# A hybrid attention and recurrence layer on one core: row spreads through DRAM in place of a matmul, and the first gate maps loaded at a written place

## The chip, the cores and the metric

The kernel runs on one NeuronCore of a Trainium2 chip. Its time is device time in microseconds (us) for one execution. The median of three runs before the change is 661.3 us (661.18 to 662.85). The core has five engines with queues of their own: TensorE (in the profile PE, its weight loads PEld), VectorE (DVE), ScalarE (ACT), GpSimd (POOL) and SyncE (SP, which here only issues transfers). Transfers are issued by SP, ACT or POOL and carried out by 16 DMA engines. An engine works its queue in order, and an instruction that waits holds up what is queued behind it on that engine.

## The reference, cut to what matters

One layer of an encoder over 512 tokens of width 2048, in float32. Three places of it need one factor per token, an inverse root of a mean square:

```python
def rms_norm(x, w):
    xf = x.astype(jnp.float32)
    y = xf * lax.rsqrt(jnp.mean(xf * xf, axis=-1, keepdims=True) + EPS)
    return (y * w.astype(jnp.float32)).astype(x.dtype)
...
    h = rms_norm(x, norm_w)
    proj = jnp.einsum('bsd,de->bse', h, w_in)
    q, k, v, g_attn, xr, g_lru = jnp.split(proj, SPLITS, axis=-1)
    attn_out = attention_group(q, k, v, q_norm_w, k_norm_w)
    lru_out = lru_group(xr, conv_w, conv_b, lru_wa, lru_ba, lru_wx, lru_bx, lru_lambda)
    mixed = jnp.concatenate([rms_norm(attn_out, attn_norm_w) * jax.nn.silu(g_attn),
                             rms_norm(lru_out, lru_norm_w) * jax.nn.silu(g_lru)], axis=-1)
    return x + jnp.einsum('bse,ed->bsd', mixed, w_out)
```

`lru_group` is a short convolution along the tokens, then two linear recurrences (forward and backward) whose gates come from block-diagonal 128x128 maps `lru_wa` and `lru_wx`, eight blocks in each direction. `attention_group` is attention of 8 query heads and 2 key heads of 128 with norms and a rotation.

## The kernel before, in words

Products are made from float32 values split in a high and a low part, three matmuls for each product (`mm3`, L144 to L147). A weight block of 256 rows by 512 columns (512 KB) is loaded into one of three raw buffers (`wraw`, L187, transfer at L193) and split by ScalarE (high part, L204) and VectorE (low part, L205); a raw buffer comes free when its split is done. A projection whose output features lie on the partitions (`proj_feat`, L278) holds four accumulators `pj` of 128x512 and runs over eight chunks c of 256 input rows; a step (c, e) is one chunk into accumulator e, six matmuls. A second projection of the kind takes the same four accumulator banks over, so its first matmul on bank e waits until the first one's bank e has been read.

The input is used without its own norm factor. x is loaded in chunks (L223), turned by TensorE (L230), scaled by the gain and split (L232, L233), and its squares are summed per token on VectorE (`xsquare`, L239). The factor `rstd` per token goes on later, when accumulators are emptied: `evac_bc` (L360 to L368) multiplies bank e, which has features on the partitions and tokens along the row, by `rbc`, a 128x512 tile that has the 512 factors on every partition.

Three times a column form of factors, [128, 4] with token 128 t + p at (p, t), has to become such a tile. That is `rows` (L262): VectorE makes four products of the identity with a column (L265), which gives a 128x512 tile with the factors on diagonals, TensorE multiplies a matrix of ones with it in float32 (L267), and VectorE copies the accumulator out (L268). The three calls:

- `xstats` (L270 to L274): VectorE adds up the sums (L272), GpSimd forms the root with two operations (`rsqrt_mean`, L256 and L257), and `rows` fills `rbc`. It is called in the main loop over the first projection's steps behind step (7, 0) (L969 to L971).
- in `kv` (L546 to L548): the squares of the recurrence output are summed over the features by `group_rstd` (L639 to L651), matmuls of 128x128 with one column of ones (L644), for two halves of `hsum`; VectorE copies the four columns out (L649), GpSimd forms the root `r_l`, four steps later `rows` fills `gbc`. `normed` (L655, L656) multiplies the recurrence outputs `hs` by it.
- at L1042, behind the attention: the same for the attention's one sum (`asum`) and root `r_a`, into the same `gbc`; L656 multiplies the attention outputs `av` by it.

The recurrence comes in two halves of four blocks (`lru_half`, L370). It first loads its four pairs of gate maps (L376 and L377, 128 KB each) into buffers of tag `k2`, then empties the accumulators with `evac_bc` (L366), and for each pair of blocks runs the split of the maps (L391, L392), the convolution (L396, L401), the gate matmuls, and the scans. `weave` mixes the next projection's steps into this chain.

What sets the order: TensorE's order is as written for the whole kernel. SP's is as written up to the end of the first projection (`s1`, closed at L973) and in the last stage, ScalarE's and VectorE's as written until step (1, 2) (`s2`, L964) and in the last stage, GpSimd's as written during the attention. Everywhere else a planner puts the instructions of an engine in order at build time, by a priority (`high_priority`) and modelled times. The gate maps of the first half are issued by `lru_half` behind L973, with a high priority, so the planner places them on SP's queue.

Of the kernel before, what the change touches and what calls it, by code (L numbers as in the profile page):

```python
# [1 line left out]

# [8 lines left out]
F32 = mybir.dt.float32  # L11
F32R = mybir.dt.float32r
AF = mybir.ActivationFunctionType
ALU = mybir.AluOpType
AX = mybir.AxisListType

P = 128
SEQ = 512
DM = 2048
KT = DM // P  # L20
NT = SEQ // P
# [34 lines left out]
def hybrid_kernel(  # L56
# [20 lines left out]
    nc = tc.nc  # L77
# [4 lines left out]
    pools, order = {}, {"left": [], "right": []}  # L82

    def opened(name, side):
        pools[name] = tc.alloc_tile_pool(name=name, bufs=1, side=side, reuse_waits="tile")
        order[side].append(name)
        return pools[name]
# [16 lines left out]
    dp = ctx.enter_context(tc.tile_pool(name="dp", bufs=1, space=bass.MemoryType.DRAM))  # L104
# [3 lines left out]
    def nm(s):  # L108
        cnt[0] += 1
        return f"{s}_{cnt[0]}"  # L110
# [4 lines left out]
    def work():  # L115
        return ("lru", LRU_K2, LRU_B4) if "lru" in pools else ("att", ATT_K2, ATT_B4)

    def k2(dt=F32, shape=(P, SEQ)):
        pool, n, _ = work()
        return pools[pool].tile(list(shape), dt, tag="k2", bufs=n, name=nm("k2"))  # L120
# [14 lines left out]
    def mm():  # L135
        return ps.tile([P, SEQ], F32, tag="mm", name=nm("mm"))

    def const(shape, name, dt=F32):
        return cp.tile(list(shape), dt, tag=name, name=name)

    def f(ap):
        return ap.bitcast(F32)
# [7 lines left out]
    ident = const([P, P], "ident")  # L150
    make_identity(nc, ident)
    ones = const([P, P], "ones")
# [64 lines left out]
    def xload(c, nk=1):  # L217

        xc = b4(shape=(P, NT, 2 * P))
        for k in range(nk):  # L220
            ks = slice(k * 2 * P // nk, (k + 1) * 2 * P // nk)
            cs = slice(c * 2 * P + ks.start, c * 2 * P + ks.stop)
            nc.sync.dma_start(xc[:, :, ks], xf[:, cs].rearrange("(t p) d -> p t d", p=P))  # L223
            yield xc

    def xturn(xc, kk):
        pt = mm()
        for t in range(NT):
            ks = slice(kk % 2 * P, (kk % 2 + 1) * P)
            nc.tensor.transpose(pt[:, t * P : (t + 1) * P], xc[:, t, ks], ident)  # L230
        xh[kk], xl[kk] = x2(), x2()
        nc.scalar.activation(xh[kk], pt, AF.Identity, scale=nw[:, kk : kk + 1])  # L232
        nc.vector.scalar_tensor_tensor(  # L233
            xl[kk], pt, nw[:, kk : kk + 1], f(xh[kk]), op0=ALU.mult, op1=ALU.subtract
        )

    def xsquare(xc, c):
        for t in range(NT):
            nc.vector.scalar_tensor_tensor(  # L239
                xc[:, t, :], xc[:, t, :], 1.0, xc[:, t, :], op0=ALU.mult, op1=ALU.mult,  # L240
                accum_out=ssq[:, t, c : c + 1],
            )

    def xchunk(c):
        with tc.high_priority(AHEAD):
            (xc,) = xload(c)
        yield
        with tc.high_priority(AHEAD):
            for k in range(2):
                xturn(xc, 2 * c + k)  # L250
        xsquare(xc, c)
        yield

    def rsqrt_mean(dst, src, n, width):

        nc.gpsimd.tensor_scalar(dst, src, 1.0 / n, EPS, op0=ALU.mult, op1=ALU.add)  # L256
        nc.gpsimd.tensor_tensor(dst, dst, nhalf[:, :width], op=ALU.pow)  # L257

    rstd = const([P, NT], "rstd")
    rbc = const([P, SEQ], "rbc")  # L260

    def rows(dst, col, dg):  # L262

        for t in range(NT):
            nc.vector.tensor_scalar(dg[:, t, :], ident, col[:, t : t + 1], None, op0=ALU.mult)  # L265
        pb = mm()
        nc.tensor.matmul(pb, ones, dg.rearrange("p t q -> p (t q)"), start=True, stop=True)  # L267
        nc.vector.tensor_copy(dst, pb)  # L268

    def xstats():  # L270
        s = const([P, NT], "xsum")
        nc.vector.reduce_sum(s, ssq, axis=AX.X)  # L272
        rsqrt_mean(rstd, s, DM, NT)
        rows(rbc, rstd, k2(shape=(P, NT, P)))  # L274

# [80 lines left out]
    sums = {}  # L358

    def evac_bc(acc):  # L360

        res = []
        with tc.high_priority():
            for a in acc:
                e = ev()
                nc.vector.tensor_mul(e, a, rbc)  # L366
                res.append(e)
        return res  # L368

    def lru_half(half, acc):  # L370

        grs = []
        for n in range(4 * half, 4 * half + 4):
            gr = k2(shape=(P, 4, P))
            with tc.high_priority(AHEAD):
                nc.sync.dma_start(gr[:, 0:2, :], lru_wa[:, n].rearrange("d c e -> c d e"))  # L376
                nc.sync.dma_start(gr[:, 2:4, :], lru_wx[:, n].rearrange("d c e -> c d e"))  # L377
            grs.append(gr)
        xrs = evac_bc(acc)
        for b in range(0, 4, 2):  # L380
            bs = slice(b, b + 2)
            steps = ((6, 4, 8, 4), (10, 5, 8, 5))[half][bs]
            yield from lru_pair(4 * half + b, xrs[bs], grs[bs], steps, 99 if half and b else 0)
# [68 lines left out]
    def lru_squares():  # L452

        hsum = pools["rot"].tile([P, 2, SEQ], F32, tag="hsum", name="hsum")
        nc.scalar.activation(hsum, hp[0], AF.Square)
        for pair in hp[1:]:
            yield 2
            sq = pools["rot"].tile([P, 2, SEQ], F32, tag="hsq", bufs=1, name=nm("hsq"))
            nc.scalar.activation(sq, pair, AF.Square)
            nc.vector.tensor_add(hsum, hsum, sq)  # L460
        sums["l"] = [hsum[:, k, :] for k in range(2)]


    def rope_consts():
# [54 lines left out]
    def turn(rot, h):  # L519

        pt = mm()
        for t in range(NT):
            nc.tensor.transpose(pt[:, t * P : (t + 1) * P], rot[t][:, h, :], ident)  # L523
        return pt

    def split_ps(pt, hi, lo):
        nc.scalar.copy(hi, pt)
        nc.vector.tensor_sub(lo, pt, f(hi))

    def kv(es):  # L530
        rot = norm_rope(es, NKV, rk)
        yield 20
        opened("wx", "right")
        for t in range(NT):
            vv = es[t][:, NKV * HD :]
            vt = pools["qkv"].tile([P, 2, NKV * HD], F32R, tag="v", bufs=NT, name=nm("v"))
            vh[t], vl[t] = vt[:, 0, :], vt[:, 1, :]
            nc.scalar.copy(vh[t], vv)
            nc.vector.tensor_sub(vl[t], vv, f(vh[t]))
        yield from lru_squares()  # L540
        for h in range(NKV):
            yield (16, 4)[h]
            kt = pools["qkv"].tile([P, 2, SEQ], F32R, tag="kt", bufs=NKV, name=nm("kt"))
            kth[h], ktl[h] = kt[:, 0, :], kt[:, 1, :]
            split_ps(turn(rot, h), kth[h], ktl[h])
        r = group_rstd(sums["l"], "r_l", NB * P)  # L546
        yield 4
        rows(gbc, r, pools["rope"].tile([P, NT, P], F32, tag="kv", bufs=NT, name=nm("kv")))  # L548

    def turned(rot, h):  # L550

# [84 lines left out]
    def fin_s(shape=(P, SEQ)):  # L636
        return pools["fin"].tile(list(shape), F32, tag="s", bufs=2, name=nm("s"))
# [15 lines left out]
    gbc = const([P, SEQ], "gbc")  # L653
# [268 lines left out]
    def busy(n):  # L922
        for _ in range(n):
            nc.tensor.matmul(warm[:, : 2 * P], wv[:, :P], wv, start=True, stop=True)
# [10 lines left out]
    with tc.high_priority():  # L935
# [8 lines left out]
        xturn(xc, 0)  # L944
        busy(WARM2)
    chunks = [xchunk(c) for c in range(1, KT // 2)]
    loads, turns = iter(chunks), iter(chunks)
    for step in proj_feat(C_XR, a1, first, given):
        if step is None:
            with tc.high_priority():  # L950
                first.append(wsplit(raw, 1))
                xturn(xc, 1)
            xsquare(xc, 0)
            next(next(loads), None)
            given[1] = wload(w_in, 2 * P, C_XR)
            continue
        c, e = step
        if (e == 0 or e == 2) and c:
            next(next(loads, iter(())), None)
        if (e, c) == (2, 0) or (e == 1 and c) or (e, c) in ((3, 1), (3, 2)):  # L960
            next(next(turns, iter(())), None)
        if (c, e) == (1, 2):
            given[2] = wload(w_in, 4 * P, C_XR)
            s2.close()  # L964
        if (c, e) == (2, 3):
            vec_load()
        if (c, e) == (5, 3):
            columns(vec, vec_st)
        if (c, e) == (KT // 2 - 1, 0):  # L969
            with tc.high_priority():  # L970
                xstats()  # L971

    s1.close()  # L973
    lru_consts()
# [28 lines left out]

    fill = both()
    weave(fill, kv(kvs))
    drain(fill)

# [29 lines left out]
    r = group_rstd([sums["a"]], "r_a", NH * HD)  # L1037
    closed("att", "qkv")
    opened("fin", "right")
    for _ in range(3):  # L1040
        next(fill)
    rows(gbc, r, fin_s((P, NT, P)))  # L1042


    def build(i, pair, where):
# [22 lines left out]
    acc = []  # L1068
# [74 lines left out]
```

## Time and profile before

| | |
|---|---|
| runs before | 661.18, 661.3, 662.85 us; median 661.3 |
| profiled execution | 660.07 us, of which 658.3 us are its span, first to last instruction |
| mean granted TensorE clock | 0.998 of full speed |
| matmuls L145 to L147 and L891, the weight products | 376 of each of the three kinds at some 0.39 us recorded in the projections with features on the partitions, 192 of each in the others, 672 in the output |
| GpSimd | 14% busy, 121 instructions |
| transfers | 96.17 MB, mean 146 GB/s |

How the lines of a profile are read: a group line names the source line, the engine, the operation, `out<-in` tiles, the shape and type, the count, then busy time and mean duration in ns. A timeline line has the start in us from the span's start, the duration in us, the engine, the line and the operation; in brackets stands how long the engine had been idle and what ended that. "Lq" engines such as SPq are the issuing queues. A line in the list of waits names who waited for whom, then us in total, the number of times and the longest. For transfers the line gives the count, KB each, and the median us from issue to landing. Matmuls are pipelined, so that a recorded matmul of 0.39 us overlaps the next one, which starts 0.23 us after it.

### The profile page before, as it was taken

What the parts mean: (1) busy time and instruction counts of PE and PEld (TensorE: products, weight loads), DVE (VectorE), ACT (ScalarE), POOL (GpSimd) and SP (SyncE); (2) the same over time, 40 slices, a digit from 0 to 9 for tenths busy, and PEclk for the clock granted to TensorE, in tenths of its full rate; (3) what the DMA queues carried; (4) which work ended last, traced back from release to release, by engine and by line L of the source; (5) the groups of instructions that cost most, each with busy time, mean ns of one, the idle gap of its engine ahead of it and who ended that gap; (6) DMA issues with size and microseconds to landing.
All of it is one profiled execution on the core that took longest, in us unless ns stands there. A gap on an engine that the chain in (4) does not pass through costs nothing.

```text
span 658.3 us, 8625 instructions
## 1 busy us (share of the span) xinstructions
PE 651.0 (99%) x2971; PEld 534.1 (81%) x2971; DVE 488.2 (74%) x843; ACT 345.6 (53%) x639; POOL 92.1 (14%) x121
## 2 busy tenths in 40 slices
PE   8999999999999999999999999999999999999997
PEld 6888888888888888888888888888888888888875
DVE  5879688977687952855955568439958998698994
ACT  3533898489856515453744446435444564334441
POOL 0000000000022301233443335410000000000000
PEclk9999999999999999999999999999999999999999
DMA  8843252322334321346875768663355766585322
GB/s 291 288 131 93 65 167 65 97 64 67 93 121 135 92 69 32 102 143 154 179 186 138 192 141 199 158 140 95 96 177 199 259 210 237 189 293 181 132 77 96
DMA packets 52731, 96.17 MB, mean 146 GB/s; under 512 B 4184, under 2 KB 14544, under 8 KB 52560
## 3 DMA queue, kind: packets, MB, share of 16 engines
q1 hardware_dynamic: 45648, 75.17, 36.1%
q0 software_dynamic: 6720, 19.93, 13.1%
q10 hardware_dynamic: 320, 0.53, 0.3%
q8 instruction: 23, 0.38, 0.2%
q14 instruction: 20, 0.16, 0.1%
HBM read 91.42 MB, written 20.97 MB: 171 GB/s over the span
## 4 chain that ended last, share of the span: by engine, by line
PE 96%; DVE 1%; DMA 1%; issue 1%; ACT 0%; ACTq 0%; DVEq 0%
PE pj L145 20%; PE pj L147 20%; PE pj L146 20%; PE mm L891 12%; PE pj L891 9%; PE mm L145 3%; PE mm L147 3%; PE mm L146 3%; PE mm L575 2%; PE mm L230 1%; PE pj L287 1%; PE mm L523 1%; DMA nw_st<-in_norm_w_dram 1%; DVE ol L706 0%; DMA rw<-in_w_out_dram 0%
## 5 line engine op out<-in xcount | busy, mean ns | idle before, releaser
L145 PE MATMUL pj<-x,wh 128*128 128x512 f32 x376 | 151.2, 402 | 0.0
L147 PE MATMUL pj<-x,wl 128*128 128x512 f32 x376 | 146.9, 391 | 0.0
L146 PE MATMUL pj<-x,wh 128*128 128x512 f32 x376 | 146.6, 390 | 0.0
L204 ACT CAST wh<-wr 128x512 fp32r<-128x512 f32 x144 | 86.5, 617 | 77.1 <-PE pj L147 28.8
L205 DVE TENSOR_TENSOR wl<-wr,wh 128x512 fp32r<-128x512 f32 x144 | 98.0, 701 | 30.3 <-ACT wh L204 30.3
L147 PEld LDWEIGHTS pj<-x,wl 128*128 128x128 f32 x376 | 70.6, 188 | 15.3
L146 PEld LDWEIGHTS pj<-x,wh 128*128 128x128 f32 x376 | 70.8, 188 | 13.9 <-issue 0.5
L145 PEld LDWEIGHTS pj<-x,wh 128*128 128x128 f32 x376 | 70.7, 188 | 13.8 <-issue 0.5
L145 PE MATMUL pj<-wh,x 128*128 128x512 f32 x192 | 75.6, 394 | 0.0
L147 PE MATMUL pj<-wh,x 128*128 128x512 f32 x192 | 75.2, 392 | 0.0
L146 PE MATMUL pj<-wl,x 128*128 128x512 f32 x192 | 75.1, 391 | 0.0
L705 ACT CAST oh<-rw 128x512 fp32r<-128x512 f32 x94 | 54.8, 618 | 31.6 <-PE mm L891 16.5
L706 DVE TENSOR_TENSOR ol<-rw,oh 128x512 fp32r<-128x512 f32 x94 | 60.5, 685 | 9.7 <-ACT oh L705 8.8
L891 PE MATMUL mm<-ol,mh 128*128 128x512 f32 x128 | 50.3, 393 | 0.5 <-DVE ol L706 0.5
L891 PE MATMUL mm<-oh,mh 128*128 128x512 f32 x128 | 50.2, 392 | 0.0
L891 PE MATMUL mm<-oh,ml 128*128 128x512 f32 x128 | 50.2, 392 | 0.0
L577 ACT CAST pt<-mm 128x512 fp32r<-128x512 f32 x32 | 18.8, 586 | 53.1 <-PE mm L575 53.1
L145 PEld LDWEIGHTS pj<-wh,x 128*128 128x128 f32 x192 | 36.1, 188 | 8.1 <-issue 0.2
L146 PEld LDWEIGHTS pj<-wl,x 128*128 128x128 f32 x192 | 36.1, 188 | 8.0 <-issue 0.2
L147 PEld LDWEIGHTS pj<-wh,x 128*128 128x128 f32 x192 | 36.0, 188 | 7.9
L563 DVE TENSOR_REDUCE mx<-mm 128x1 f32<-128x512 f32 x32 | 22.1, 689 | 24.5 <-PE mm L147 24.0
L891 PE MATMUL pj<-ol,mh 128*128 128x512 f32 x96 | 37.9, 394 | 0.0
(207 smaller groups left out, 1112.0 us busy)
## 6 DMA issues: line engine op xcount, KB each, us to landing
wr<-in_w_in_dram SPq DMA_DIRECT2D x71, 512.0 KB, 3.7
rw<-in_w_out_dram SPq DMA_DIRECT2D x63, 256.0 KB, 3.7
ts<-in_w_out_dram POOLq DMA_DIRECT2D x24, 512.0 KB, 6.7
rw<-ts SPq DMA_DIRECT2D x31, 256.0 KB, 4.6
ts<-ts POOLq DMA_DIRECT2D x8, 512.0 KB, 5.3
xt<-in_x_dram SPq DMA_DIRECT2D x8, 512.0 KB, 8.7
b<-in_x_dram SPq DMA_DIRECT2D x7, 512.0 KB, 7.6
out_dram<-xt POOLq DMA_DIRECT2D x12, 256.0 KB, 3.0
```

What stands on the lines that cost most here:

```text
L145: nc.tensor.matmul(acc, lh, rh, start=start, stop=False)
L146: nc.tensor.matmul(acc, lh, rl, start=False, stop=False)
L147: nc.tensor.matmul(acc, ll, rh, start=False, stop=stop)
L204: nc.scalar.copy(hi, raw[:, k, :])
L205: nc.vector.tensor_sub(lo, raw[:, k, :], f(hi))
L230: nc.tensor.transpose(pt[:, t * P : (t + 1) * P], xc[:, t, ks], ident)
L563: nc.vector.tensor_reduce(mx, sc, axis=AX.X, op=ALU.max, negate=True)
L575: nc.tensor.transpose(pt[:, s * P : (s + 1) * P], p[:, s * P : (s + 1) * P], ident)
L577: nc.scalar.copy(pth[:, :, tt], p3)
L705: nc.scalar.copy(hi, src)
L706: nc.vector.tensor_sub(lo, src, f(hi))
L891: nc.tensor.matmul(bank[name, s], lh[:, a, ts_], rh, start=i == 0 and j == 0, stop=i == 7 and j == 2,)
```

## The change

`rows` loses the diagonal products, the matmul of ones and the 128x512 copy. In their place TensorE turns the [128, 4] column form to [4, 128] with one transpose, VectorE copies that into a small tile `line_sb`, GpSimd stores it to DRAM as one line of 512 values, and a second GpSimd transfer reads that line into all 128 partitions of the target. `xstats` becomes a generator in two parts: the sum and the root are written behind step (6, 0), and `rows` behind (6, 1), where the old call stood behind (7, 0). The loads of the first half's gate maps become a generator too, of which two maps are taken behind (6, 0) and two behind (6, 1), that is in the stretch in which SP's order is as written; the second half's are loaded where they were. In `lru_squares` VectorE adds the two halves of `hsum` into one, so that `group_rstd` has one part to sum over instead of two.

```diff
--- before.py
+++ after.py
@@ -1,3 +1,4 @@
+import itertools
 from contextlib import ExitStack
 
 import numpy as np
@@ -259,19 +260,23 @@
     rstd = const([P, NT], "rstd")
     rbc = const([P, SEQ], "rbc")
 
-    def rows(dst, col, dg):
-
-        for t in range(NT):
-            nc.vector.tensor_scalar(dg[:, t, :], ident, col[:, t : t + 1], None, op0=ALU.mult)
-        pb = mm()
-        nc.tensor.matmul(pb, ones, dg.rearrange("p t q -> p (t q)"), start=True, stop=True)
-        nc.vector.tensor_copy(dst, pb)
+    line_sb = const([NT, P], "line_sb")
+
+    def rows(dst, col):
+
+        pt = mm()
+        nc.tensor.transpose(pt[:NT, :P], col, ident)
+        nc.vector.tensor_copy(line_sb, pt[:NT, :P])
+        line = dp.tile([1, SEQ], F32, tag=nm("line"), bufs=1, name=nm("line"))
+        nc.gpsimd.dma_start(line.rearrange("o (t p) -> (o t) p", p=P), line_sb)
+        nc.gpsimd.dma_start(dst, line.broadcast_to([P, SEQ]))
 
     def xstats():
         s = const([P, NT], "xsum")
         nc.vector.reduce_sum(s, ssq, axis=AX.X)
         rsqrt_mean(rstd, s, DM, NT)
-        rows(rbc, rstd, k2(shape=(P, NT, P)))
+        yield
+        rows(rbc, rstd)
 
 
 
@@ -367,15 +372,20 @@
                 res.append(e)
         return res
 
-    def lru_half(half, acc):
-
-        grs = []
+    gate_maps = {}
+
+    def gate_loads(half):
+
         for n in range(4 * half, 4 * half + 4):
             gr = k2(shape=(P, 4, P))
             with tc.high_priority(AHEAD):
                 nc.sync.dma_start(gr[:, 0:2, :], lru_wa[:, n].rearrange("d c e -> c d e"))
                 nc.sync.dma_start(gr[:, 2:4, :], lru_wx[:, n].rearrange("d c e -> c d e"))
-            grs.append(gr)
+            yield gr
+
+    def lru_half(half, acc):
+
+        grs = gate_maps.pop(half, None) or list(gate_loads(half))
         xrs = evac_bc(acc)
         for b in range(0, 4, 2):
             bs = slice(b, b + 2)
@@ -458,7 +468,8 @@
             sq = pools["rot"].tile([P, 2, SEQ], F32, tag="hsq", bufs=1, name=nm("hsq"))
             nc.scalar.activation(sq, pair, AF.Square)
             nc.vector.tensor_add(hsum, hsum, sq)
-        sums["l"] = [hsum[:, k, :] for k in range(2)]
+        nc.vector.tensor_add(hsum[:, 0, :], hsum[:, 0, :], hsum[:, 1, :])
+        sums["l"] = [hsum[:, 0, :]]
 
 
     def rope_consts():
@@ -545,7 +556,7 @@
             split_ps(turn(rot, h), kth[h], ktl[h])
         r = group_rstd(sums["l"], "r_l", NB * P)
         yield 4
-        rows(gbc, r, pools["rope"].tile([P, NT, P], F32, tag="kv", bufs=NT, name=nm("kv")))
+        rows(gbc, r)
 
     def turned(rot, h):
 
@@ -944,6 +955,7 @@
         xturn(xc, 0)
         busy(WARM2)
     chunks = [xchunk(c) for c in range(1, KT // 2)]
+    stats, maps = xstats(), gate_loads(0)
     loads, turns = iter(chunks), iter(chunks)
     for step in proj_feat(C_XR, a1, first, given):
         if step is None:
@@ -966,9 +978,10 @@
             vec_load()
         if (c, e) == (5, 3):
             columns(vec, vec_st)
-        if (c, e) == (KT // 2 - 1, 0):
+        if c == KT // 2 - 2 and e in (0, 1):
             with tc.high_priority():
-                xstats()
+                next(stats, None)
+            gate_maps.setdefault(0, []).extend(itertools.islice(maps, 2))
 
     s1.close()
     lru_consts()
@@ -1039,7 +1052,7 @@
     opened("fin", "right")
     for _ in range(3):
         next(fill)
-    rows(gbc, r, fin_s((P, NT, P)))
+    rows(gbc, r)
 
 
     def build(i, pair, where):
```

## The prediction, made before the changed kernel was run

> **What bounds the kernel now.** I read the page first (busy times, then the chain that ended last), then TensorE's list of waits.
>
> ```profile
> span 658.3 us, 8625 instructions
> ...
> PE 651.0 (99%) x2971; PEld 534.1 (81%) x2971; DVE 488.2 (74%) x843; ACT 345.6 (53%) x639; POOL 92.1 (14%) x121
> ...
> PE 96%; DVE 1%; DMA 1%; issue 1%; ACT 0%; ACTq 0%; DVEq 0%
> ```
>
> ```profile
> PE mm L179 <- DMA nw_st<-in_norm_w_dram: 1.4, 1, 1.4
> PE mm L924 <- POOL ones L153: 1.1, 1, 1.1
> PE mm L891 <- DVE ol L706: 0.5, 1, 0.5
> ```
>
> TensorE is busy for 651.0 of 658.3 us, holds 96% of the chain, and waits three times for 3.0 us in all. So a microsecond of matmul taken away is a microsecond of time, as long as no new wait appears; what other engines or transfers save is worth nothing by itself. Two of the waits lie at the start, ahead of everything that changes; only the last 0.5 us could also go. The profiled execution took 660.07 us: its span of 658.3 and 1.77 around it. The median of the runs before, 661.3, lies 1.23 above that. I work out a difference against the profiled run and put it on the median.
>
> **What TensorE loses.** The spreading matmul at L267, at its three places, in the timeline. In steady flow a 128x512 matmul starts 0.23 us after the one before it (53.28, 53.51):
>
> ```profile
> 53.28 0.40 PE L147 MATMUL pj<-x,wl 128*128 128x512 f32 x1
> 53.51 1.02 PE L267 MATMUL mm<-k,ones 128*128 128x512 f32 x2
> ...
> 54.61 0.39 PE L146 MATMUL pj<-x,wh 128*128 128x512 f32 x1
> ...
> 239.05 1.02 PE L267 MATMUL mm<-kv,ones 128*128 128x512 f32 x2
> 240.14 0.39 PE L146 MATMUL pj<-wl,x 128*128 128x512 f32 x1
> ...
> 448.17 1.02 PE L267 MATMUL mm<-s,ones 128*128 128x512 f32 x2
> 449.26 0.39 PE L146 MATMUL pj<-x,wh 128*128 128x512 f32 x1
> ```
>
> Without L267, the L146 matmul would start one pitch after L267's place. It starts 1.10, 1.09 and 1.09 us after it, so each call costs 0.87, 0.86 and 0.86 us: 2.59 in all. (The recorded 1.02 us overlaps its neighbours; the displacement of what follows is the price.) Each call becomes one transpose. The nearest row is the transpose of 104 rows, priced in the same way:
>
> ```profile
> 46.57 0.25 PE L179 MATMUL mm<-ident,vec_st 104*128 104x104 f32 x1
> ...
> 46.91 0.39 PE L146 MATMUL pj<-x,wh 128*128 128x512 f32 x1
> ```
>
> 46.91 - 46.57 - 0.23 = 0.11 us; three cost 0.33. The new one has only four columns to turn but streams 128 columns of identity; 0 and 0.87 (as now) are the far ends, and I take 0.11, the row of the same operation. Net: 2.59 - 0.33 = 2.26 us.
>
> The sums of squares of the recurrence group go from two halves to one, L644 from 16 instructions to 8. The attention group's call has 8 already and gives the price:
>
> ```profile
> 231.70 1.84 PE L644 MATMUL mm<-ones,hsum 128*128 128x1 f32 x16
> 233.41 0.48 PE L145 MATMUL pj<-wh,x 128*128 128x512 f32 x1
> ...
> 443.14 0.95 PE L644 MATMUL mm<-ones,asum 128*128 128x1 f32 x8
> 443.95 0.47 PE L145 MATMUL pj<-x,wh 128*128 128x512 f32 x1
> ```
>
> To the next matmul it is 1.71 us against 0.81: a gain of 0.90, less at most some 0.03 for the join; I take 0.87. TensorE's work falls by 2.26 + 0.87 = 3.1 us, 0.47%.
>
> **What may give it back: the first spread.** In place of matmul and copy stand a copy of 4x128, a GpSimd transfer to DRAM, and a second GpSimd transfer that cannot be issued until the first has landed. TensorE's next projection takes over the four accumulators of the first one, so its first matmul waits until VectorE has emptied accumulator 0 (L366), which needs rbc.
>
> ```profile
> 42.59 1.04 POOL L257 TENSOR_TENSOR rstd<-rstd,nhalf 128x4 f32<-128x4 f32 x1
> ...
> 47.12 0.26 DVE L181 COPY vec<-mm 128x104 f32<-128x104 f32 x1
> ...
> 55.30 1.36 DVE L366 TENSOR_TENSOR ev<-pj,rbc 128x512 f32<-128x512 f32 x2
> ...
> 58.49 0.39 PE L145 MATMUL pj<-x,wh 128*128 128x512 f32 x1
> ```
>
> The call now stands behind step (7,0), the 53.28 row being that step's last. Moved behind (6,1), it goes forward by three steps of six matmuls, 18 x 0.227 = 4.1 us, to 49.4 us; rstd is done at 43.6, so TensorE does not wait there. The old kernel's next projection starts at 58.49, 18 matmuls behind L267's place. Without L267 but with a transpose it can start at 58.49 - 0.87 + 0.11 = 57.7. From there I go back: 0.1 for a semaphore and 0.68 for one emptying (half of the 1.36), so rbc must have landed by 56.9. Forward: the copy of the vector row came 0.55 us after its transpose had begun and took 0.26, so line_sb is full at 49.4 + 0.55 + 0.26 = 50.2, and GpSimd, idle here, issues at 50.3. With 0.1 between the transfers, their two landings together may take 56.9 - 50.3 - 0.1 = **6.5 us**; beyond that TensorE stands still microsecond for microsecond. The trace has neither transfer. The rows near them, each with KB and median from issue to landing, and the line under GpSimd's stores (minimum, median, maximum):
>
> ```profile
> out_dram<-xt POOLq DMA_DIRECT2D x12, 256.0 KB, 3.0
> ...
> rw<-in_w_out_dram SPq DMA_DIRECT2D x63, 256.0 KB, 3.7
> ...
> rw<-ts SPq DMA_DIRECT2D x31, 256.0 KB, 4.6
> ...
> ts<-in_w_out_dram POOLq DMA_DIRECT2D x24, 512.0 KB, 6.7
> ```
>
> ```profile
> DMA to landing us min/median/max: 2.5/3.0/5.3
> ```
>
> ```profile
> 1.20 4.10 DMA nw_st<-in_norm_w_dram
> ```
>
> The line of 2 KB goes the way of the 256 KB stores, so I take their minimum, 2.5; the spread writes 256 KB to 128 partitions out of DRAM like the rw loads, so 3.7. Sum 6.2, inside 6.5 by 0.3: no stall, but thin cover. Bounds: 2.5 + 2.5 = 5.0 at the low end (which gains nothing more, since TensorE does not wait here now), 4.1 (the one small load of the trace that ends on the chain, taken while the transfers were crowded) + 4.6 = 8.7 at the high one. For the low side speaks that the 16 transfer engines are only 0.37 busy here (49.5 to 57.7 us; the row gives span, the busy time of TensorE, its weight loads, VectorE, ScalarE and GpSimd, the clock, the transfer engines' share and GB/s):
>
> ```profile
> 49.50:57.70 8.20, 8.20 (x36) 6.43 (x35) 7.33 (x27) 2.06 (x3) 0.00 (x0) 1.00 0.37 120
> ```
>
> VectorE, 7.33 of 8.20 us busy in that stretch, stands behind the first L366 and starts about a microsecond later than now, but it drops four products and a copy of 128x512; what it feeds next, the splits for the second chunk, is needed only 24 matmuls (5.5 us) after 57.7.
>
> [...]
>
> **The other two spreads, and the loads.** Nothing waits for them early:
>
> ```profile
> 258.38 0.19 POOL L256 TENSOR_SCALAR rr<-rr 128x4 f32<-128x4 f32 x1 [23.26 <-ACT sh L498]
> ...
> 545.60 0.66 POOL L826 DMA_DIRECT2D out_dram<-xt  x1 [99.54 <-DVE xt L862]
> ```
>
> ```profile
> 240.84 2.36 DVE L656 TENSOR_TENSOR hs<-hs,gbc 128x1024 f32<-128x1024 f32 x2
> ...
> 464.86 1.22 DVE L656 TENSOR_TENSOR av<-av,gbc 128x1024 f32<-128x1024 f32 x1
> ```
>
> ```profile
> 248.00:252.00 4.00, 4.00 (x19) 3.25 (x18) 0.69 (x1) 0.62 (x1) 0.00 (x0) 1.00 0.23 51
> ```
>
> The two transposes stand where L267 stands now, at 239.05 and 448.17; TensorE does not wait there today (no L267 in its list), although the matmul needs the root and four products of it, and the transpose needs the root alone. GpSimd stands still between its two transfers, with nothing queued behind it until 258.4 and 545.6. The first gbc lands some 7 us after its transpose, near 246, where VectorE now starts at 240.84; that work moves into a stretch in which VectorE has little to do (0.69 of 4 us from 248 to 252, the third busy time of the row), and if it had no such cover it would cost 4.7 us (four of half 2.36). The third lands near 455; VectorE reaches L656 at 464.9. The added join of the two halves is one VectorE addition of 128x512, 0.7 us, more than 20 us ahead of L644. Taken at nothing, all three.
>
> The gate maps, on the sync queue:
>
> ```profile
> 25.25 0.37 SPq L193 DMA_DIRECT2D wr<-in_w_in_dram  x1
> 29.45 0.37 SPq L193 DMA_DIRECT2D wr<-in_w_in_dram  x1
> ...
> 37.16 2.00 SPq L376 DMA_DIRECT2D k<-in_lru_wa_dram  x4
> ...
> 45.85 1.30 ACT L204 CAST wh<-wr 128x512 fp32r<-128x512 f32 x2 [4.13 <-PE pj L146]
> ```
>
> By the order written, the eight issues come between the weight loads of chunks 6 and 7 and, at 2.00 us for four, run from 25.7 to 29.7; chunk 7's load slips from 29.45 to 29.7. Its split starts at 45.85 and waits for TensorE, not for data: 12 us of cover over a landing of 3.7 to 8. Worth nothing in either direction.
>
> **Rivals.** A difference below 0.3%, 2.0 us, is about what a measurement of this kernel cannot tell from no change.
>
> A, the spread comes late: with 4.1 + 4.6 = 8.7 us for the pair, TensorE stalls 2.2 us at the hand-over and the gain shrinks to 0.9: 660.4. For it speaks the thin cover, and that weight loads use the same engines in this stretch; against it that share of 0.37. It counts as "same" from a pair of 7.6 us (a stall of 1.1) on.
>
> B, slower: the same wait, with each transfer landing like GpSimd's 512 KB transfers, 6.7 us. The pair takes 13.4, the stall is 6.9 and the result +3.8: 665.1. It decides from a pair of 11.6 us on (6.5 + 3.1 + 2.0). Against it: those move 256 times the bytes of the line, and none of GpSimd's 12 stores needed over 5.3.
>
> C, the planner gives VectorE another order here, so that two of its 0.69 us operations run ahead of the first emptying: with the pair at 6.2 that is a stall of 1.1, and the time 659.3. Nothing in the profile speaks for it; the profile can't exclude it, since VectorE's order here is not written by hand.
>
> D, GpSimd itself is slow to issue. Its DRAM-to-DRAM transfers (L736) took this long on the engine (minimum, median, maximum in ns):
>
> ```profile
> L736 POOL DMA_DIRECT2D ts<-ts x8: 553/583/1617, 324.2 to 422.0; - x8
> ```
>
> Twice the excess over the median, 2 x 1.03 us, puts the pair at 8.3: a stall of 1.8 and 660.0. [...]
>
> **How the numbers follow.** Forecast, no stall to speak of: 0.62, a gain of 3.1: 657.0 on the profiled run's scale, 658.2 on the median's. A 0.20, C 0.06, D 0.04: together 0.30 for "same". B 0.08. The low end takes the profiled run's scale and the 0.5 us wait away: 657.0 - 0.5 = 656.5; the high end is a stall of 3.1, all the gain, at 661.3.
>
> **What the changed profile must show.** L267 gone, three transposes, L644 with 16 instructions instead of 24, and TensorE's busy time down by about 3 us. The first L366 starts at 56 to 57 us. TensorE's list of waits holds the three old entries and no entry for L145 behind L366 near 57.7. The gate maps issue from 25.7 on. I am wrong if that L145 waits a microsecond or more, or if TensorE waits for a split further on.

## The result, and the profile after

The changed kernel takes 657.49 us (median of six runs, 656.88 to 658.22) against 661.58 us (six runs, 661.17 to 662.85). The ratio is 0.9940, with a 95% interval of 0.9926 to 0.9954, so the gain is between 3.0 and 4.9 us. A second measurement, in another job (`a0_after` below), gave 658.86 against 661.59: ratio 0.9961, interval 0.9949 to 0.9974. The predicted 3.1 us (a ratio of 0.9953) lies in both intervals.

The page of the changed kernel, then TensorE's list of waits:

```profile
span 655.3 us, 8600 instructions
...
PE 647.8 (99%) x2960; PEld 532.1 (81%) x2960; DVE 485.8 (74%) x832; ACT 344.4 (53%) x639; POOL 96.5 (15%) x127
```

```profile
PE mm L180 <- DMA nw_st<-in_norm_w_dram: 1.5, 1, 1.5
PE mm L935 <- POOL ones L154: 1.1, 1, 1.1
PE mm L902 <- DVE ol L717: 0.5, 1, 0.5
```

The span is 3.0 us shorter, TensorE's busy time 3.2 us, and the three waits are the old three. TensorE waits at none of the new transfers. The timeline of the first spread (start, duration, both in us; in brackets the idle time before and what ended it):

```profile
49.57 0.27 PE L268 MATMUL mm<-ident,rstd 128*4 128x128 f32 x1
...
50.12 0.27 DVE L269 COPY line_sb<-mm 4x128 f32<-4x128 f32 x1
...
50.71 0.72 POOL L271 DMA_DIRECT2D line<-line_sb  x1 [5.47 <-DVE lc L353]
...
52.74 0.60 POOL L272 DMA_DIRECT2D rbc<-line  x1 [1.31 <-DMA line<-line_sb]
...
56.27 1.89 DVE L371 TENSOR_TENSOR ev<-pj,rbc 128x512 f32<-128x512 f32 x3 [1.82 <-DMA rbc<-line]
```

```profile
57.63 0.39 PE L148 MATMUL pj<-x,wl 128*128 128x512 f32 x1
57.86 0.39 PE L146 MATMUL pj<-x,wh 128*128 128x512 f32 x1
```

rbc landed at 56.2. VectorE had waited 1.82 us for it, emptied the first accumulator by 56.9 (a third of the 1.89), and the next projection's first matmul, at 57.86, follows its forerunner at the usual pitch of 0.23: the cover left was about 0.8 us.

### The profile page after: what moved, and what is told of

Read it like the earlier page. It is cut to its first block, busy times and chain, and to the rows that moved or that the text cites. A ratio compares the mean times of both kernels' runs of the same rounds, so it can differ in the third digit from the quotient of the medians.

```text
span 655.3 us, 8600 instructions
## 1 busy us (share of the span) xinstructions
PE 647.8 (99%) x2960; PEld 532.1 (81%) x2960; DVE 485.8 (74%) x832; ACT 344.4 (53%) x639; POOL 96.5 (15%) x127
## 4 chain that ended last, share of the span: by engine, by line
PE 96%; DVE 1%; DMA 1%; issue 1%; ACT 0%; ACTq 0%; DVEq 0%
PE pj L146 20%; PE pj L148 20%; PE pj L147 20%; PE mm L902 12%; PE pj L902 9%; PE mm L146 3%; PE mm L148 3%; PE mm L147 3%; PE mm L586 2%; PE mm L231 1%; PE pj L292 1%; PE mm L534 1%; DMA nw_st<-in_norm_w_dram 1%; DVE ol L717 0%; DMA rw<-in_w_out_dram 0%
## 5 line engine op out<-in xcount | busy, mean ns | idle before, releaser
L206 DVE TENSOR_TENSOR wl<-wr,wh 128x512 fp32r<-128x512 f32 x144 | 98.7, 706 | 29.7 <-ACT wh L205 29.7
```

The lines of the kernel that those rows point to most:

```text
L206: nc.vector.tensor_sub(lo, raw[:, k, :], f(hi))
```

## The experiments

All were timed in five rounds against the kernel before on the same chip. Differences in us are worked out from the ratio and 661.5.

**The parts alone.** `a0_after` is the change again. `e1_join` is the kernel before with the joined halves only, `e11_rows` the changed kernel without them:

```diff
+        nc.vector.tensor_add(hsum[:, 0, :], hsum[:, 0, :], hsum[:, 1, :])
-        sums["l"] = [hsum[:, k, :] for k in range(2)]
+        sums["l"] = [hsum[:, 0, :]]
```

`e2_maps` is the kernel before with the gate maps at their written place, and nothing else; `e3_no_maps` is the changed kernel with the maps left to the planner (only the lines of the main loop are shown; the loads also move out of `lru_half` into a generator, and back):

```diff
 # e2_maps
 ...
+        if c == KT // 2 - 2 and e in (0, 1):
+            gate_maps.setdefault(0, []).extend(itertools.islice(maps, 2))
 # e3_no_maps
 ...
-            gate_maps.setdefault(0, []).extend(itertools.islice(maps, 2))
```

> The whole change again, beside its parts on the same chip. Theory P (the gain is TensorE's work alone): 3.1 us below the kernel before, span 3.0 to 3.1 below. Theory M (the written place of the gate maps is worth about a microsecond by itself, which would explain that the medians fell by 4.1 and the profiled spans by 3.0): 4.1 below.

> The kernel before with one edit alone: the two halves of the recurrence group's squares are added on VectorE, so that the sums over features take 8 matmul instructions instead of 16. Theory P: 0.87 us below the kernel before, with no new wait of TensorE. Theory M: the same 0.87.

> The kernel before with one edit alone: the first half's gate maps loaded in SP's written order behind steps (6,0) and (6,1). Theory P: 0.0 us from the kernel before. Theory M: 1.0 us below.

> The changed kernel without the gate maps' new place (they are loaded by the planner's order as before). Theory P: as the changed kernel, 3.1 below the kernel before. Theory M: 1.0 us above the changed kernel.

> The changed kernel without the joined sums (16 instructions at the recurrence group's sums again): spreads and maps as changed. Theory P: 0.87 us above the changed kernel and 2.2 us below the kernel before.

| | median | ratio to before, 95% interval | difference |
|---|---|---|---|
| a0_after | 658.86 | 0.9961 (0.9949 to 0.9974) | -2.6 (-3.4 to -1.7) |
| e1_join | 660.43 | 0.9980 (0.9971 to 0.9988) | -1.3 (-1.9 to -0.8) |
| e11_rows | 659.12 | 0.9969 (0.9960 to 0.9977) | -2.1 (-2.6 to -1.5) |
| e2_maps | 661.51 | 1.0004 (0.9995 to 1.0012) | +0.3 (-0.3 to +0.8) |
| e3_no_maps | 662.55 | 1.0018 (1.0009 to 1.0027) | +1.2 (+0.6 to +1.8) |

The two gains on TensorE, 1.3 and 2.1 us, agree with the expected 0.87 and 2.2 within their intervals; sharper figures stand at the end of this section. The maps' new place is worth nothing on the kernel before, and it decides the sign of the change: without it the changed kernel is slower than the kernel before. Neither theory had that; P held for four of the five, M fell with e2_maps. TensorE's waits in e3_no_maps have a new first entry, and its sync queue begins otherwise than the changed kernel's:

```profile
PE mm L231 <- DMA b<-in_x_dram: 4.2, 1, 4.2
```

```profile
0.73 1.97 SPq L381 DMA_DIRECT2D k<-in_lru_wa_dram  x4
2.75 2.75 SPq L382 DMA_DIRECT2D k<-in_lru_wx_dram  x4
5.54 1.57 SPq L224 DMA_DIRECT2D b<-in_x_dram  x3
```

The eight map loads, which the kernel before issued at 37 to 41 us, now stand ahead of everything, and x, which TensorE needs first, is issued 4.8 us later than in the kernel before, whose sync queue begins so:

```profile
0.73 1.54 SPq L223 DMA_DIRECT2D b<-in_x_dram  x3
```

In the changed kernel the written place holds them back (first and last of eight, then the weight load behind them):

```profile
26.09 0.46 SPq L382 DMA_DIRECT2D k<-in_lru_wa_dram  x1
...
31.85 0.37 SPq L383 DMA_DIRECT2D k<-in_lru_wx_dram  x1
32.32 12.13 SPq L194 DMA_DIRECT2D wr<-in_w_in_dram  x3
```

**Why the loads jump forward.** The maps' buffers have the tag `k2`, a ring of 12, and so had the diagonal tile of the old first spread, which was taken from the ring ahead of them. Two kernels test whether that tile was what held the loads back:

```diff
 # e8_hold: e3_no_maps with a k2 buffer taken and written behind the first spread
         rows(rbc, rstd)
+        hold = k2(shape=(P, NT, P))
+        nc.vector.tensor_scalar(hold[:, 0, :], ident, rstd[:, 0:1], None, op0=ALU.mult)
 # e9_other_ring: the kernel before, its diagonal tile from another ring
-        rows(rbc, rstd, k2(shape=(P, NT, P)))
+        rows(rbc, rstd, b4(shape=(P, NT, P)))
```

> The changed kernel with the maps left to the planner (as in e3_no_maps), but with a k2 buffer taken in the first spread, ahead of the maps' buffers, and one product of the identity with the root written to it, as the old diagonal products did (nothing reads it). In e3_no_maps the planner issued the eight map loads first of all, from 0.73 us, and TensorE waited 4.2 us for the first x chunk. Theory K (the old diagonal tile stood ahead of the maps in the ring of k2 buffers and so held their loads back until the root was known; the change took it away, and the written place puts a bound in its stead): the loads go out near 37 us, no wait for x, time as the changed kernel, some 4.4 us below e3_no_maps. Rival L (the loads go early for another reason, such as the transfer times in the planner's model): loads first, time as e3_no_maps.

> The kernel before with one edit: the diagonal products of the first spread go to a buffer of tag b4 in place of one of tag k2; the work is the same. Theory K: the maps' loads go out first, from 0.7 us, TensorE waits some 4.2 us for the first x chunk, and the time is about 4.4 us above the kernel before, near 666. Rival L: no difference.

e8_hold: 657.63, ratio 0.9952 (0.9938 to 0.9965), 3.2 us below the kernel before: the whole gain is back. Its loads go out late again:

```profile
38.46 2.00 SPq L383 DMA_DIRECT2D k<-in_lru_wa_dram  x4
```

e9_other_ring: 666.04, ratio 1.0077 (1.0063 to 1.0092), 5.1 us above the kernel before (4.2 to 6.1), though it does the same work. Its sync queue and TensorE's wait are those of e3_no_maps:

```profile
0.73 2.00 SPq L376 DMA_DIRECT2D k<-in_lru_wa_dram  x4
```

```profile
PE mm L230 <- DMA b<-in_x_dram: 4.3, 1, 4.3
```

So it is shown from both sides that a `k2` buffer taken in the first spread, ahead of the maps' buffers, keeps their high-priority loads behind the x loads. When the buffer goes, something else has to. One part of theory K does not hold as it is worded: on the chip the loads do not wait for the root. In e8_hold they go out from 38.46 us, and the buffer is written 7 us later:

```profile
45.59 0.29 DVE L281 TENSOR_SCALAR k<-ident,rstd 128x128 f32<-128x128 f32 x1 [1.22 <-POOL rstd L258]
```

In the kernel before they go out from 37.16, and the root is done at 43.6. What the buffer changes is the place in SP's queue that the planner gives the loads when the kernel is built. By which rule it does so, and whether a buffer that has nothing to do with the root would serve as well, no run shows.

**The cover of the first spread.** `e4_late` and `e5_late2` are the changed kernel with the first spread written behind (7, 0) and (7, 2):

```diff
         if c == KT // 2 - 2 and e in (0, 1):
-            with tc.high_priority():
-                next(stats, None)
+            if e == 0:
+                with tc.high_priority():
+                    next(stats, None)
             gate_maps.setdefault(0, []).extend(itertools.islice(maps, 2))
+        if (c, e) == (KT // 2 - 1, 0):   # (KT // 2 - 1, 2) in e5_late2
+            with tc.high_priority():
+                next(stats, None)
```

> The changed kernel with the first spread written behind step (7,0), where the old one stood, 18 matmuls or 4.1 us later. In the changed kernel's trace the transpose starts at 49.57 and the first emptying of an accumulator at 56.27; 4.1 later that is 60.4, its end 61.0, and the next projection can start at 57.8. Theory H (hand-over: rbc is what the next projection waits for, cover some 0.8 us): TensorE waits 3.2 to 3.3 us there, the time is 3.2 us above the changed kernel, about that of the kernel before. Rival N (the wait is hidden anyway, since other work or another wait ends last there): no wait, time as the changed kernel.

> The same with the first spread behind step (7,2), 12 matmuls or 2.7 us later still. Theory H: TensorE waits 6.0 us, the time is 6.0 above the changed kernel and some 2.5 above the kernel before: each microsecond past the cover costs one. Rival N: as the changed kernel.

e4_late: 664.94, ratio 1.0051 (1.0035 to 1.0068), 3.4 us above the kernel before and so 6.5 above the changed kernel, with 3.1 us for its gain. e5_late2: 667.82, ratio 1.0093 (1.0080 to 1.0106), 6.2 above the kernel before, 9.3 above the changed one. TensorE's wait is where theory H put it; e4_late's, then e5_late2's:

```profile
PE pj L146 <- DVE ev L371: 4.6, 1, 4.6
```

```profile
PE pj L146 <- DVE ev L371: 6.3, 1, 6.3
```

Rival N is out. But e4_late waited 4.6 us, not 3.3, since its two transfers took longer: its first issue at 56.12 to the first emptying at 63.05 is 6.9 us, against 5.6 in the changed kernel. And both cost more than their waits. e4_late's TensorE behind the wait:

```profile
63.89 0.60 PE L146 MATMUL pj<-x,wh 128*128 128x512 f32 x1 [4.64 <-DVE ev L371]
64.29 0.63 PE L147 MATMUL pj<-x,wh 128*128 128x512 f32 x1
...
67.28 0.49 PE L148 MATMUL pj<-x,wl 128*128 128x512 f32 x1
67.61 0.39 PE L146 MATMUL pj<-x,wh 128*128 128x512 f32 x1
67.84 0.40 PE L147 MATMUL pj<-x,wh 128*128 128x512 f32 x1
```

From 63.89 to 67.28 eight matmuls start 0.42 us apart in place of 0.23: 3.4 us for what takes 1.8, a loss of 1.6 us on top of the wait, together 6.2. In e5_late2, twelve matmuls go at that rate (65.77 to 71.03), a loss of 2.5: together 8.8. A wait also pushes its matmul 0.16 us further than its idle time says, since that is counted from the recorded end of the matmul before, 0.39 us after its start, where the next one would have started after 0.23. So the sums are 6.4 and 9.0, which agrees with the measured 6.5 and 9.3.

**The matmul put back, and a spread without TensorE.** `e6_both` adds the float32 matmul of ones again beside each new spread; `e7_column` stores the column form value by value:

```diff
 # e6_both, in rows, behind the second transfer
+        pb = mm()
+        nc.tensor.matmul(pb, ones, f(xh[0]), start=True, stop=True)
+        nc.vector.tensor_copy(spare, pb[:, :1])
 # e7_column
-        pt = mm()
-        nc.tensor.transpose(pt[:NT, :P], col, ident)
-        nc.vector.tensor_copy(line_sb, pt[:NT, :P])
-        nc.gpsimd.dma_start(line.rearrange("o (t p) -> (o t) p", p=P), line_sb)
+        nc.gpsimd.dma_start(line.rearrange("o (t p) -> p (o t)", p=P), col)
```

> The changed kernel with a float32 matmul of 128x512 by the matrix of ones put back behind each of the three transposes; its result is not used, only one column of it is copied out. Theory P: 2.6 us above the changed kernel (three times 0.87), TensorE's list of waits unchanged. If the matmul were worth less than its displacement in the trace, less; if the spread through DRAM cost anything elsewhere, the difference from the kernel before would not be the 0.87 of the joined sums less 0.33 for the transposes, 0.5 us below it.

> The changed kernel without transpose and copy: GpSimd stores the [128,4] column form straight to DRAM, 512 values of 4 bytes each, and reads the line back into 128 partitions. Three transposes less, 0.33 us below the changed kernel by theory P, if the store of 4-byte pieces lands in time; the first spread no longer stands in TensorE's order and starts when the root is done, near 43.6, so up to 9 us more for the store cost nothing. Rival: the store of single values takes so long (over 9 us) that TensorE waits at the hand-over.

e6_both: 662.93, ratio 1.0022 (1.0012 to 1.0033), 1.5 us above the kernel before: 4.6 over the changed kernel where 2.6 were expected. At its place the matmul costs what was expected; in e6_both's timeline

```profile
50.85 1.02 PE L275 MATMUL mm<-x,ones 128*128 128x512 f32 x2
51.31 0.79 PE L146 MATMUL pj<-x,wh 128*128 128x512 f32 x1
51.94 0.39 PE L147 MATMUL pj<-x,wh 128*128 128x512 f32 x1
```

51.94 - 50.85 - 0.23 = 0.86 us, and the list of waits has the same three entries. The other 2 us are spread out: with the three spreads left aside, TensorE falls behind the changed kernel by some 0.6 us between 62 and 203 us and by 0.9 between 243 and 444 (the mean distance of single matmuls is 231 ns against 229 from 300 to 400). What causes that was not found. Laid side by side, the two traces part in many steps of some 9 ns, from 66.7 us on mostly at matmuls into an accumulator `mm` and at the first ones into `pj` behind them. e6_both takes one `mm` more for each spread, which shifts the buffer that every later one gets; that is a candidate, but the order of VectorE differs a little too, and no run separates the two.

e7_column: 661.48, ratio 0.9999 (0.9991 to 1.0008), no gain at all. The rival held:

```profile
45.63 0.95 POOL L267 DMA_DIRECT2D line<-rstd  x1 [0.32 <-POOL rstd L258]
55.65 0.57 POOL L268 DMA_DIRECT2D rbc<-line  x1 [9.08 <-DMA line<-rstd]
```

```profile
PE pj L146 <- DVE ev L367: 3.3, 2, 2.4
```

The store of 512 single values takes 10.0 us to the next issue, where the same 2 KB in rows of 512 bytes take 2.0 (50.71 to 52.74). rbc came at 60.9 and TensorE waited 3.3 us in two pieces, about the 3.1 of the change and the 0.33 of the three transposes together. Behind the longer piece its matmuls are back at their usual distance almost at once:

```profile
61.81 0.47 PE L146 MATMUL pj<-x,wh 128*128 128x512 f32 x1 [2.39 <-DVE ev L367]
62.11 0.40 PE L147 MATMUL pj<-x,wh 128*128 128x512 f32 x1
62.35 0.39 PE L148 MATMUL pj<-x,wl 128*128 128x512 f32 x1
```

**The start.** `e10_warm` is the changed kernel with five more warming matmuls ahead of TensorE's first transposes:

```diff
-WARM, WARM2 = 13, 6
+WARM, WARM2 = 18, 6
```

> The changed kernel with 18 warming matmuls at the start in place of 13 (their results are not used). In two profiles of the changed kernel the first group of four L292 matmuls took 1.20 us in one and 2.06 in the other, and the spans differ by 1.8 (655.3 and 657.1). Theory S (the runs differ because TensorE stands idle from 4.1 to 5.5 us ahead of its first transposes and then runs on at half its rate in some executions): with the gap filled every run falls in the fast group, 656.9 to 657.2. Rival: the five more matmuls delay the first transposes, or the spread of the runs stays.

657.03 us, all runs from 656.96 to 657.51, ratio 0.9943 (0.9931 to 0.9955): the steadiest version, and no slower than the changed kernel, whose twelve runs go from 656.88 to 659.50, four of them as low as these five. What differs among those twelve shows in the chains of the two profiles of the changed kernel, the first, then the one of a0_after:

```profile
7.12 1.20 PE pj L292 x4
...
8.75 3.21 PE pj L292 x14
```

```profile
8.15 1.71 PE pj L292 x4
...
10.52 3.19 PE pj L292 x14
```

The 1.8 us between the spans, 655.3 and 657.1, are there at 10 us already (10.52 - 8.75), and the rest of the two executions is alike. (The 2.06 us of the expectation are the timeline's; the chain counts 1.71, from the end of the piece before.) Theory S fits: the idle time ahead of the first transposes is cut from 1.5 to 0.5 us (the changed kernel, then e10_warm), and all five runs took as little as the shortest four of the changed kernel:

```profile
5.55 0.20 PE L180 MATMUL mm<-ident,nw_st 16*128 16x16 f32 x1 [1.46 <-DMA nw_st<-in_norm_w_dram]
```

```profile
5.49 0.20 PE L180 MATMUL mm<-ident,nw_st 16*128 16x16 f32 x1 [0.51 <-DMA nw_st<-in_norm_w_dram]
```

The edit also makes the busy stretch ahead of the gap longer, 3.9 us in place of 3.0, and no run separates the two. The spread of the start belongs to the kernel before too, whose runs in these jobs go from 659.96 to 662.76, so that a median of a few runs can lie a microsecond off.

**The runs with the start taken off.** The chain of every profile has a mark behind the start: the last group of the first chunk's matmuls, six of them (the kernel before, then the changed one):

```profile
12.71 1.38 PE pj L287 x6
```

```profile
12.83 1.38 PE pj L292 x6
```

From that mark to the end of the span, one profiled execution each:

| | mark at, us | mark to end, us | against the kernel before |
|---|---|---|---|
| the kernel before | 12.71 | 645.6 | |
| the changed kernel | 12.83 | 642.5 | -3.1 |
| a0_after | 14.59 | 642.5 | -3.1 |
| e1_join | 14.70 | 644.7 | -0.9 |
| e11_rows | 14.48 | 643.3 | -2.3 |
| e2_maps | 14.12 | 645.7 | +0.1 |
| e3_no_maps | 18.32 | 642.5 | -3.1 |
| e8_hold | 14.42 | 642.8 | -2.8 |
| e9_other_ring | 17.92 | 645.6 | 0.0 |
| e4_late | 14.07 | 648.9 | +3.3 |
| e5_late2 | 14.31 | 651.5 | +5.9 |
| e6_both | 13.99 | 647.1 | +1.5 |
| e7_column | 14.36 | 645.9 | +0.3 |
| e10_warm | 12.77 | 642.5 | -3.1 |

The joined sums are worth 0.9 us, the spreads 2.3, the maps' place by itself nothing. What e3_no_maps and e9_other_ring lose lies wholly ahead of the mark, which they reach 5.5 and 5.2 us later than the kernels that they were made from. e4_late and e5_late2 lose 6.5 and 9.0 against the changed kernel.

## Why the prediction was right, and what it missed

**TensorE's work, 3.1 us.** Right, and best seen with the start taken off. The kernel before reaches its group of 14 at 8.63 us:

```profile
8.63 3.21 PE pj L287 x14
```

From there to the end it takes 658.3 - 8.63 = 649.7 us; the changed kernel takes 646.5 and a0_after 646.6: 3.1 less. That the two measurements gave 4.0 and 2.6 us by their ratios is the spread of the start, and so are the 1.23 us that the forecast carried from the profiled run to the median. The single terms agree as well. The transposes cost what the 104-row transpose did:

```profile
237.53 0.27 PE L268 MATMUL mm<-ident,r_l 128*4 128x128 f32 x1
...
237.87 0.39 PE L147 MATMUL pj<-wl,x 128*128 128x512 f32 x1
```

237.87 - 237.53 - 0.23 = 0.11. The joined sums:

```profile
231.07 0.95 PE L655 MATMUL mm<-ones,hsum 128*128 128x1 f32 x8
231.88 0.48 PE L146 MATMUL pj<-wh,x 128*128 128x512 f32 x1
```

0.81 us to the next matmul, as priced from the attention's call, against 1.71 before.

**The hand-over.** Right, with the two transfers sized a little too long: 2.0 us from the first issue to the second and 3.5 from there to the emptying, 5.6 in all, against the 6.2 taken and the 6.5 allowed. The issue came 0.4 us later than worked out: from the end of the copy to it passed 0.3 us at each of the three spreads, where 0.1 had been taken. Over the three spreads the store landed after 1.7 to 4.1 us and the spread after 3.4 to 4.4, so the bounds of 5.0 and 8.7 for a pair held, and rival A was near: the third pair had both maxima, 8.5, which at the first spread would have cost some 2 us. Rival C did not come, since VectorE stood idle for 1.82 us ahead of the first emptying, and of rival D's slow issues there was none: GpSimd's six took 0.58 to 0.72 us each. Rival B needed 11.6 us; e5_late2 shows its mechanism, and its price was set too low, because it counted the wait alone and not the slower matmuls behind it.

**The other two spreads** cost nothing, as said, though with less to spare. The first gbc came at 244.4; VectorE waited 3.1 us for it, and TensorE did not notice. The second landed at 459.0, not near 455, and VectorE, in another order than before, took it up at 460.2, not at 464.9: a cover of one microsecond where ten were worked out.

```profile
244.39 3.50 DVE L667 TENSOR_TENSOR hs<-hs,gbc 128x1024 f32<-128x1024 f32 x3 [3.12 <-DMA gbc<-line]
...
460.18 1.22 DVE L667 TENSOR_TENSOR av<-av,gbc 128x1024 f32<-128x1024 f32 x1
```

**The step that failed: the gate maps, "Worth nothing in either direction".** The step compared the maps' new place with their old one and was right in that (e2_maps: +0.3, interval across zero, and +0.1 from the mark; the eight issues took 6.1 us and not 4.0, and chunk 7's load slipped to 32.3 and not to 29.7, without effect). But the old place was not on offer any more. The working asked of each removed piece what time it took, and not what it held: the diagonal tile had a place in a ring of buffers, and the planner's freedom with the loads hung on it. Left out, the maps' place would have turned 3 us gained into 1 us lost (e3_no_maps). None of the rivals had this. The forecast came out right because the change itself provided for it, not because the reasoning saw it: here it was lucky.

## What to carry to other kernels

In a kernel whose one engine is busy 99% of the time, price a removed instruction by how far it pushes the next one on that engine, and price what replaces it by the time from which another engine would wait; here both were good to a few tenths of a microsecond. Before a buffer is removed, look up what is allocated behind it in the same ring and with what priority: an unneeded tile can be all that keeps an early load from going first. TensorE's waits of 4.6 and 6.3 us cost 1.6 and 2.5 us beyond their length, since the matmuls behind them were slower, and a wait of 2.4 us did not. A start that differs from run to run can hide a gain of this size, and a mark behind it in the profile takes it off. At the kernel's start, idle time ahead of the first real matmuls can be filled with matmuls whose result nobody reads, which here made the time of five runs steadier (656.96 to 657.51 us, against 656.88 to 659.50 in the twelve of the changed kernel).

## What the runs showed of the hardware

Behind waits of 4.6 and 6.3 us TensorE took 3.4 and 5.3 us to come back to its rate, at 0.42 us for a matmul that else starts every 0.23. Behind e7_column's wait of 2.4 us the distances were 0.30, 0.24 and then 0.23. The profile's granted clock tells the same behind the longest wait, 0.50 from 66 to 70 us in e5_late2 (the columns are span, busy times of TensorE, its weight loads, VectorE, ScalarE and GpSimd, the clock, the share of the transfer engines, GB/s):

```profile
66.00:70.00 4.00, 4.00 (x10) 3.13 (x11) 3.49 (x6) 0.86 (x2) 0.00 (x0) 0.50 0.00 0
```

It does not tell it everywhere. In a0_after matmuls start 0.43 us apart from 8.38 to 9.66 us, and the clock stands at 1.00:

```profile
8.00:10.00 2.00, 2.00 (x7) 1.51 (x7) 0.98 (x2) 0.10 (x1) 0.00 (x0) 1.00 1.08 373
```

In e8_hold its mean over the span is 0.946, and the stretch from the mark to the end takes 642.8 us, where the changed kernel takes 642.5 with a clock of 1.00. In these traces the starts of the matmuls are the surer measure of the rate.

Why the rate fell behind the waits of 4.6 and 6.3 us and not behind the one of 2.4, and what sets the start, which differs from run to run (the marks lie at 12.7 to 14.7 us in the kernels that do not wait for x), no run shows.
